# Gate logits and branch products with columns on partitions, and the merged sum split straight from SBUF

## The chip, the core and the metric

The kernel runs on one core of one Trainium2 chip. The metric is device time in microseconds (us), from launch to end, as the median of several runs. The engines are TensorE (PE; its weight loads are listed apart as PEld), VectorE (DVE), ScalarE (ACT), GpSimd (POOL) and SyncE (SP), which issues the large transfers.

## The reference

Two layers of a streaming encoder on x of 256 tokens by 2048 channels, all in float32. What bears on the change:

```python
proj = h @ w_in                       # 2048 -> 14400 columns
(rq, rk, rv, rg, lx, lg, mq, mkv, mkr, mg, merge_logits) = split(proj, ...)
gates  = sigmoid(merge_logits).reshape(256, 3, 2048)
merged = (gates[:, 0] * (y_ret @ w_branch[0:1024])
        + gates[:, 1] * (y_lru @ w_branch[1024:2048])
        + gates[:, 2] * (y_mla @ w_branch[2048:3072]))
y   = merged @ w_out
out = x + (1 + res_gate) * rms_norm(y, norm_post)
```

`h` is a normalised x, scaled and shifted by vectors that come from `silu(c) @ ada_w` (2048 by 6144 per layer; this sum is called ada below).

## The kernel before

**Products.** Every large product takes its weights in tiles of 256 rows by 1024 columns. A tile is one transfer of 1 MB on SP's queue into a buffer called raw (four of them, shared with the loads of ada_w). It is cut into two pieces of 128 rows by 1024 columns, kt 0 and kt 1. ACT rounds each piece to a 12-bit head, `wh` (line 291), and DVE subtracts the head to get the rest, `wl` (line 292). There are three `wh` and three `wl` buffers in all. The activation is kept in the same two parts, `h` and `l`. A product is the sum of three matmuls, wh by h, wh by l and wl by h.

A product can be made in two ways. With **tokens on partitions** (`gemm_x`, line 349) the activation is stationary and the weights are moving, 128 rows by 512 columns: 24 matmuls per tile. In the last tile of a group its steps are sorted by token half, so that the two PSUM banks of the first half are complete before those of the second. With **columns on partitions** (`gemm_w`, lines 367 to 369) the weights are stationary and the activation is moving, 128 by 256 tokens: 48 matmuls per tile, kt 0 first and kt 1 after it in every tile. A group is a product of 1024 columns. It takes four of the six PSUM banks called acc; two more banks, called mi, serve small work. Its results are read out of the four banks, an eviction for each: ACT by a copy (line 392) or a sigmoid (line 398), DVE by an add to a partial sum (line 394).

**Stages of a layer.** Layer 0 computes h in blocks of 2, 2, 4, 4 and 4 pieces of 128 channels, as its shift and scale become known, and after each block multiplies it into six groups called lx, lg, mqkv, mg, lru0 and lru1. In the first two blocks each group is thus a single tile, and in the other three it is two tiles. lx, lg and mg have columns on partitions. lru0 and lru1 are the two halves of the gate logits of the LRU branch and have, like all logits, tokens on partitions. The remaining products follow: those of retention and of MLA, with groups of 8 tiles, and the logits mla0, mla1, ret0, ret1. In layer 1 every group of `w_in` has 8 tiles. The six branch products (`branch`, 4 tiles each) multiply their PSUM banks by the gates on DVE (line 1047) and add them on POOL (line 1050). The sum is then transposed, 64 transposes of 128 by 128 through the mi banks (line 1105), and split into the two parts (lines 567 on ACT and 568 on DVE) for the product with `w_out`.

**Order.** PE and SP work in program order: small work (attention, transposes, sums over partitions) is called between tiles by `tick`. The order on ACT, DVE and POOL is made by a scheduler at build time, from priorities; casts and subtractions of weights come first (offset 400), then evictions (offset 300). On the chip each engine then works its list in order. The sums for ada (line 454 on DVE, line 445 on ACT, line 449 on POOL) run on tiles of ada_w beside the products: shift and scale of layer 0 during its first blocks, and its residual gate and the sums for layer 1 later, through the rest of layer 0.

Of the kernel before, what the change touches and what calls it, by code (L numbers as in the profile page):

```python
# [14 lines left out]
AF = mybir.ActivationFunctionType  # L15
# [4 lines left out]
P = 128  # L20
# [18 lines left out]
# per-layer vectors and their 128-blocks (ada_b: shift and scale only)  # L39
# [14 lines left out]
def hybrid_trunk(ctx: ExitStack, tc: tile.TileContext, a, out):  # L54
# [178 lines left out]
    def softplus_lambda(l):  # L233
        """8 * softplus(-lambda), and its negative"""
# [38 lines left out]
    def load_split(src, nk, ncol, spare=None):  # L273
        """heads and rests of a tile [128, nk, ncol], at most 1024 columns in a piece; in slots, listed in
        spare, if that is given"""
# [26 lines left out]
    class Act:  # L302
        """An operand [d, tokens], head and rest, in pieces of four d-tiles."""
# [21 lines left out]
    def gemm_x(act, w, r0, c0, kts, banks, ncol=W1, before=None, late=False):  # L325
        """tokens on partitions: banks[hf][j] += act.T @ w, the d-tiles in kts; yields after each tile.
        The first half of the tokens ends ahead of the second, by two tiles with late."""
# [25 lines left out]
    def gemm_w(act, w, r0, c0, kts, banks, before=None):  # L353
        """columns on partitions: banks[j][:, n, :] += w.T @ act for 8 blocks of 128 columns."""
        k_all = list(range(*kts))
        for k0 in k_all[::2]:
            nk = min(2, kts[1] - k0)
            if before is not None:
                before(k0)
            for k, (wh, wl) in enumerate(load_split(wsrc(w, r0, k0, nk, c0, W1), nk, W1)):  # L360
                kt = k0 + k
                for nb in range(8):
                    dst = banks[nb // 2][:, (nb % 2) * T:(nb % 2 + 1) * T]
                    cs = slice(nb * P, (nb + 1) * P)
                    first = kt == k_all[0] and nb % 2 == 0
                    last = kt == k_all[-1] and nb % 2 == 1
                    mm(dst, wh[:, cs], act.H(kt), start=first, stop=False, skip_group_check=True)  # L367
                    mm(dst, wh[:, cs], act.L(kt), start=False, stop=False, skip_group_check=True)  # L368
                    mm(dst, wl[:, cs], act.H(kt), start=False, stop=last, skip_group_check=True)  # L369
            yield  # L370
# [5 lines left out]
    def act_slice(res, i):  # L376
        """The i-th 512 columns of a result held in two slots."""
        return res[i // 2][:, (i % 2) * 512:(i % 2 + 1) * 512]

    def group(act, w, c0, mode, kts, res, func, partial, before):  # L380
        """One product of 1024 columns into two slots (res, if given): token halves, or blocks 0-3 and 4-7."""
# [28 lines left out]
    def mean_of(ss):  # L410
        """sum of the parts / D + eps"""
# [5 lines left out]
    def square(src, acc, vector=False):  # L417
        """acc: the row sums of src ** 2, 512 columns"""
# [43 lines left out]
    def ada_block(l, k0, k1, pause, share):  # L462
        """gain and shift of the d-tiles k0..k1"""
# [14 lines left out]
    def gains(l, scale, shift, k0, k1):  # L478
        """norm gain and shift of the d-tiles k0..k1 from the adaLN sums."""
# [17 lines left out]
    def ada_res(l):  # L497
        """(1 + res_gate) * norm_post on every partition, in pieces of 512 columns"""
# [762 lines left out]
```

## Time and profile before

| | |
|---|---|
| median of 3 runs (lowest, highest) | 2019.5 us (2019.4, 2023.18) |
| the profiled execution: span | 2016.0 us |
| its own time, span and what lies around it | 2019.5 us, the median, stands for it: 3.5 us lie outside the span |
| PE matmul busy | 1932.3 us, 96%, 9980 matmuls |
| PE weight loads busy | 1624.1 us, 81% |
| DVE busy | 1399.9 us, 69% |
| ACT busy | 991.0 us, 49% |
| POOL busy | 181.6 us, 9% |
| mean granted clock of TensorE | 0.991 |

The page gives one profiled execution. The span is the time from its first to its last instruction; the time of a run is longer by what lies ahead of and behind that. In a row of the timeline the first number is the start, the second the duration in us, and square brackets hold the idle time before the instruction and what ended it. A row with x2 or more stands for several instructions on end.

### The profile page before, as it was taken

How to read it: one execution, taken by the hardware profiler on the slowest of the kernel's cores; microseconds unless marked ns; L12 is line 12 of the kernel's file. 1: busy time of each engine (PE TensorE's matmuls, PEld its weight loads, DVE VectorE, ACT ScalarE, POOL GpSimd, SP SyncE). 2: the span in 40 equal slices, each digit the busy share in tenths (PEclk: the TensorE clock that was granted, in tenths of full speed). 3: DMA queues.
4: the chain of work that ended last, by engine and by line, in shares of the span. 5: the costliest groups of instructions: out<-in, count | busy, mean ns of one | idle time of the engine just before them, and what ended most of it. 6: DMA issues, size and time to landing. Idle time of an engine off the chain costs nothing.

```text
span 2016.0 us, 25350 instructions
## 1 busy us (share of the span) xinstructions
PE 1932.3 (96%) x9980; PEld 1624.1 (81%) x9980; DVE 1399.9 (69%) x1812; ACT 991.0 (49%) x1286; POOL 181.6 (9%) x137
## 2 busy tenths in 40 slices
PE   2979999999999999999989999999999999999998
PEld 2867888778988888777879989888898888788886
DVE  7899989787877687767567754446565447786555
ACT  5744538644554544433454774444455444444443
POOL 2242401100000010102010010000000001010100
PEclk9989999999999999999989999999999999999999
DMA  8787863787867777776655555555554557778563
GB/s 294 260 285 272 304 234 120 272 291 245 297 236 252 266 255 259 277 271 217 222 198 189 173 181 188 188 178 181 171 192 147 198 186 250 246 270 282 187 210 125
DMA packets 156936, 456.98 MB, mean 227 GB/s; under 512 B 12144, under 2 KB 20336, under 8 KB 156816
## 3 DMA queue, kind: packets, MB, share of 16 engines
q1 hardware_dynamic: 153248, 443.44, 64.8%
q0 software_dynamic: 3424, 11.65, 1.9%
q8 instruction: 78, 1.28, 0.3%
q14 instruction: 42, 0.34, 0.0%
q10 hardware_dynamic: 144, 0.26, 0.0%
HBM read 451.13 MB, written 4.19 MB: 226 GB/s over the span
## 4 chain that ended last, share of the span: by engine, by line
PE 79%; DVE 11%; DMA 6%; ACT 2%; issue 2%; POOL 0%; SPq 0%; DVEq 0%; ACTq 0%; POOLq 0%
PE acc L349 59%; DMA raw<-in_ada_w 5%; DVE float L454 4%; DVE wl L292 4%; PE acc L368 4%; PE acc L369 4%; PE acc L367 4%; DVE float L394 1%; PE mi L714 1%; PE mi L713 1%; PE mi L871 1%; ACT wh L291 0%; POOL float L891 0%; DMA raw<-in_w_in 0%; PE mi L801 0%
## 5 line engine op out<-in xcount | busy, mean ns | idle before, releaser
L349 PE MATMUL acc<-wh,float32r 128*128 128x512 f32 x4064 | 1159.4, 400 | 4.7 <-DVE float L394 4.4
L292 DVE TENSOR_TENSOR wl<-raw,wh 128x1024 fp32r<-128x1024 f32 (+1 forms) x640 | 794.0, 1244 | 451.9 <-ACT wh L291 445.4
L291 ACT CAST wh<-raw 128x1024 fp32r<-128x1024 f32 (+1 forms) x640 | 666.0, 1042 | 826.0 <-PE acc L349 656.2
L349 PEld LDWEIGHTS acc<-wh,float32r 128*128 128x128 f32 x4064 | 759.2, 189 | 186.3 <-DVE float L394 8.4
L349 PE MATMUL acc<-wl,float32r 128*128 128x512 f32 x2032 | 651.8, 397 | 13.8 <-DVE wl L292 13.8
L349 PEld LDWEIGHTS acc<-wl,float32r 128*128 128x128 f32 x2032 | 381.9, 189 | 110.6 <-DVE wl L292 20.6
L454 DVE SCALAR_TENSOR_TENSOR float<-raw,c_act,float 128x512 f32<-128x512 f32 (+1 forms) x326 | 255.7, 786 | 62.6 <-DMA raw<-in_ada_w 57.9
L367 PE MATMUL acc<-float32r,wh 128*128 128x256 f32 x768 | 218.7, 285 | 5.0 <-ACT float32r L567 5.0
L368 PE MATMUL acc<-float32r,wh 128*128 128x256 f32 x768 | 217.2, 283 | 0.8 <-DVE float32r L568 0.8
L369 PE MATMUL acc<-float32r,wl 128*128 128x256 f32 x768 | 217.1, 283 | 0.7 <-DVE wl L292 0.6
L367 PEld LDWEIGHTS acc<-float32r,wh 128*128 128x128 f32 x768 | 147.2, 192 | 6.3 <-ACT float32r L567 5.8
L368 PEld LDWEIGHTS acc<-float32r,wh 128*128 128x128 f32 x768 | 147.0, 191 | 1.8 <-DVE float32r L568 1.4
L369 PEld LDWEIGHTS acc<-float32r,wl 128*128 128x128 f32 x768 | 146.9, 191 | 1.1 <-DVE wl L292 1.1
L449 POOL TENSOR_TENSOR float<-float,float 128x512 f32<-128x512 f32 (+1 forms) x49 | 70.9, 1448 | 112.5 <-ACT float L445 107.5
L1050 POOL TENSOR_TENSOR float<-float,float 128x512 f32<-128x512 f32 x32 | 52.7, 1663 | 258.5 <-DVE float L1047 243.0
L394 DVE TENSOR_TENSOR float<-acc,float 128x512 f32<-128x512 f32 x96 | 62.5, 682 | 2.8 <-PE acc L349 1.4
L445 ACT ACTIVATE float<-raw,c_act 128x512 f32<-128x512 f32 (+1 forms) x64 | 40.1, 664 | 31.6 <-DMA raw<-in_ada_w 31.5
L793 POOL DMA_DIRECT2D float<-in_ret_gn x4 | 2.3, 570 | 570.0 <-PE mi L739 371.4
L470 PE MATMUL mi<-ident,float 128*128 128x128 f32 x64 | 10.4, 303 | 41.2 <-DVE float L458 41.2
L470 PEld LDWEIGHTS mi<-ident,float 128*128 128x128 f32 x64 | 8.1, 154 | 43.4 <-DVE float L458 42.5
L398 ACT ACTIVATE float<-acc 128x512 f32<-128x512 f32 x56 | 31.7, 598 | 13.0 <-PE acc L349 12.8
L1047 DVE TENSOR_TENSOR float<-acc,float 128x512 f32<-128x512 f32 x48 | 31.8, 683 | 2.4 <-PE acc L349 2.2
(231 smaller groups left out, 1286.2 us busy)
## 6 DMA issues: line engine op xcount, KB each, us to landing
raw<-in_w_in SPq DMA_DIRECT2D x224, 1024.0 KB, 5.1
raw<-in_ada_w SPq DMA_DIRECT2D x96, 1024.0 KB, 6.9
raw<-in_w_branch SPq DMA_DIRECT2D x48, 1024.0 KB, 6.2
raw<-in_w_out SPq DMA_DIRECT2D x32, 1024.0 KB, 5.5
raw<-in_mla_w_ukv SPq DMA_DIRECT2D x8, 1024.0 KB, 6.0
raw<-in_mla_w_uq SPq DMA_DIRECT2D x8, 768.0 KB, 4.5
float<-in_x SPq DMA_DIRECT2D x8, 512.0 KB, 7.5
float<-in_k_decay POOLq DMA_DIRECT2D x4, 512.0 KB, 4.5
```

Source lines behind the costliest of these rows:

```text
L291: nc.scalar.copy(wh, raw[:, c0:c0 + n])
L292: nc.vector.tensor_tensor(out=wl, in0=raw[:, c0:c0 + n], in1=wh.bitcast(F32), op=ALU.subtract)
L349: mm(b[:, 0:w_n], x, ws[:, j * w_n:(j + 1) * w_n], start=st, stop=sp)
L367: mm(dst, wh[:, cs], act.H(kt), start=first, stop=False, skip_group_check=True)
L368: mm(dst, wh[:, cs], act.L(kt), start=False, stop=False, skip_group_check=True)
L369: mm(dst, wl[:, cs], act.H(kt), start=False, stop=last, skip_group_check=True)
L394: nc.vector.tensor_tensor(out=dst, in0=b, in1=dst, op=ALU.add)
L445: nc.scalar.activation(out=t, in_=src, func=AF.Copy, scale=c)
L449: nc.gpsimd.tensor_tensor(out=acc[1], in0=acc[1], in1=t, op=ALU.add)
L454: nc.vector.scalar_tensor_tensor(acc[0], src, c, acc[0], ALU.mult, ALU.add)
L1047: nc.vector.tensor_tensor(out=gate[hf][:, cs], in0=banks[hf][j], in1=gate[hf][:, cs], op=ALU.mult)
L1050: nc.gpsimd.tensor_tensor(out=dst, in0=dst, in1=gate[hf][:, cs], op=ALU.add)
```

## The change

1. Gate logits: their six groups of 8 tiles per layer are made with columns on partitions (`m = "w"`) where they had tokens on partitions. The gate is then laid out with columns on partitions.
2. Branch products: their six groups of 4 tiles per layer go the same way, so that gates and products fit. Multiplications and additions stay as many, each of 128 by 512.
3. The merged sum now has channels on partitions. The 64 transposes go, and the split reads the sum from SBUF where it read PSUM.
4. `gemm_w` sorts the steps of its last tile by block of 128 columns: for each block kt 0, then kt 1. This holds for all groups with columns on partitions, lx, lg and mg among them. A group that is a single tile is sorted as a whole.

Over both layers, 3456 matmuls of 128 by 512 become 6912 of 128 by 256 (6 groups of 8 tiles and 6 of 4 per layer, 24 matmuls per tile before and 48 after). Comments and docstrings are left out too; below `gemm_w` the line numbers of the changed kernel are larger by two, and by one from `branch` on.

```diff
     def gemm_w(act, w, r0, c0, kts, banks, before=None):
         k_all = list(range(*kts))
         for k0 in k_all[::2]:
...
-            for k, (wh, wl) in enumerate(load_split(wsrc(w, r0, k0, nk, c0, W1), nk, W1)):
-                kt = k0 + k
-                for nb in range(8):
-                    dst = banks[nb // 2][:, (nb % 2) * T:(nb % 2 + 1) * T]
-                    cs = slice(nb * P, (nb + 1) * P)
-                    first = kt == k_all[0] and nb % 2 == 0
-                    last = kt == k_all[-1] and nb % 2 == 1
-                    mm(dst, wh[:, cs], act.H(kt), start=first, stop=False, skip_group_check=True)
-                    mm(dst, wh[:, cs], act.L(kt), start=False, stop=False, skip_group_check=True)
-                    mm(dst, wl[:, cs], act.H(kt), start=False, stop=last, skip_group_check=True)
+            steps = [(nb, k0 + k, ws) for k, ws in enumerate(load_split(wsrc(w, r0, k0, nk, c0, W1), nk, W1)) for nb in range(8)]
+            if k0 + nk > k_all[-1]:
+                steps.sort(key=lambda s: s[0])
+            for nb, kt, (wh, wl) in steps:
+                dst = banks[nb // 2][:, (nb % 2) * T:(nb % 2 + 1) * T]
...
-                c0, func, m = logits_col(*n), AF.Sigmoid, "x"
+                c0, func, m = logits_col(*n), AF.Sigmoid, "w"
...
-            banks = [[bank() for _ in range(2)] for _ in range(2)]
-            drive(gemm_x(acts[b], a["w_branch"][l], r0, c * W1, (0, 8), banks))
-            for hf in range(2):
-                for j in range(2):
-                    cs = slice(j * 512, (j + 1) * 512)
-                    nc.vector.tensor_tensor(out=gate[hf][:, cs], in0=banks[hf][j], in1=gate[hf][:, cs], op=ALU.mult)
-                    if order:
-                        dst = macc[hf][c][:, cs]
-                        nc.gpsimd.tensor_tensor(out=dst, in0=dst, in1=gate[hf][:, cs], op=ALU.add)
+            banks = [bank() for _ in range(4)]
+            drive(gemm_w(acts[b], a["w_branch"][l], r0, c * W1, (0, 8), banks))
+            for i, b_i in enumerate(banks):
+                g = act_slice(gate, i)
+                nc.vector.tensor_tensor(out=g, in0=b_i, in1=g, op=ALU.mult)
                 if order:
-                    release(gate[hf])
-                else:
-                    macc[hf][c] = gate[hf]
+                    dst = act_slice(macc[c], i)
+                    nc.gpsimd.tensor_tensor(out=dst, in0=dst, in1=g, op=ALU.add)
...
-        def turn_merged(c):
+        def split_merged(c):
             yield 1
-            for k in range(0, 8, 2):
-                b = mbank()
-                for i in range(2):
-                    for hf in range(2):
-                        nc.tensor.transpose(b[:, i * T + hf * P:i * T + (hf + 1) * P], macc[hf][c][:, (k + i) * P:(k + i + 1) * P], ident)
-                split_to(M, c * 8 + k, 2, b)
+            for i in range(4):
+                split_to(M, c * 8 + 2 * i, 2, act_slice(macc[c], i))
                 yield 1
```

The order of DVE moves with it. The first place is the last tile of the logits group ret1 in layer 0, at 892 us of the trace: its two pieces are `wl_7370` and `wl_7374` (raw_7367), and raw_7443 is a tile of ada_w. Before:

```order
L292 TENSOR_TENSOR wl_7328<-raw_7321,wh_7327 128x1024
L292 TENSOR_TENSOR wl_7370<-raw_7367,wh_7369 128x1024
L454 SCALAR_TENSOR_TENSOR float_11_87<-raw_7443,c_act,float_11_87 128x512 x2
L292 TENSOR_TENSOR wl_7374<-raw_7367,wh_7373 128x1024
L454 SCALAR_TENSOR_TENSOR float_11_87<-raw_7443,c_act,float_11_87 128x512 x2
L292 TENSOR_TENSOR wl_7412<-raw_7409,wh_7411 128x1024
```

Of the change, the same tile is raw_8879 with the pieces `wl_8882` and `wl_8886`, and raw_9003 is the same tile of ada_w:

```order
L292 TENSOR_TENSOR wl_8816<-raw_8809,wh_8815 128x1024
L292 TENSOR_TENSOR wl_8882<-raw_8879,wh_8881 128x1024
L456 SCALAR_TENSOR_TENSOR float_11_87<-raw_9003,c_act,float_11_87 128x512 x3
L292 TENSOR_TENSOR wl_8886<-raw_8879,wh_8885 128x1024
L456 SCALAR_TENSOR_TENSOR float_11_87<-raw_9003,c_act,float_11_87 128x512
```

Three ada steps stand ahead of the tile's second `wl` where two stood; the branch product ret0, at 917 us, moves in the same way.

The second place is DVE where a two-tile group lru1 ends and the next one begins, in layer 0 at 229 us (acc_1971 to acc_1974 are the banks of the group that has ended, raw_2115 and raw_2157 the next tiles). Before:

```order
L292 TENSOR_TENSOR wl_2048<-raw_2041,wh_2047 128x1024
L292 TENSOR_TENSOR wl_2118<-raw_2115,wh_2117 128x1024
L454 SCALAR_TENSOR_TENSOR float_6_82<-raw_2149,c_act,float_6_82 128x512 x2
L394 TENSOR_TENSOR float_19_95<-acc_1971,float_19_95 128x512
L292 TENSOR_TENSOR wl_2122<-raw_2115,wh_2121 128x1024
L394 TENSOR_TENSOR float_19_95<-acc_1972,float_19_95 128x512
L394 TENSOR_TENSOR float_20_96<-acc_1973,float_20_96 128x512
L292 TENSOR_TENSOR wl_2160<-raw_2157,wh_2159 128x1024
L394 TENSOR_TENSOR float_20_96<-acc_1974,float_20_96 128x512
```

Of the change, the banks are acc_2163 to acc_2166 and the next tiles raw_2307 and raw_2349:

```order
L292 TENSOR_TENSOR wl_2240<-raw_2233,wh_2239 128x1024
L292 TENSOR_TENSOR wl_2310<-raw_2307,wh_2309 128x1024
L396 TENSOR_TENSOR float_19_95<-acc_2163,float_19_95 128x512
L456 SCALAR_TENSOR_TENSOR float_6_82<-raw_2341,c_act,float_6_82 128x512
L396 TENSOR_TENSOR float_19_95<-acc_2164,float_19_95 128x512
L456 SCALAR_TENSOR_TENSOR float_6_82<-raw_2341,c_act,float_6_82 128x512
L396 TENSOR_TENSOR float_20_96<-acc_2165,float_20_96 128x512
L396 TENSOR_TENSOR float_20_96<-acc_2166,float_20_96 128x512
L292 TENSOR_TENSOR wl_2314<-raw_2307,wh_2313 128x1024
L292 TENSOR_TENSOR wl_2352<-raw_2349,wh_2351 128x1024
```

All four evictions now stand ahead of the next tile's second `wl`, where three of them stood behind it.

The third place is ACT at the end of the first single-tile group, lx of the first block, at about 50 us. raw_316 is the tile of the group after, and acc_232 to acc_235 are the banks of the group that ends. Before:

```order
L291 CAST wh_318<-raw_316 128x1024
L445 ACTIVATE float_15_91<-raw_374,c_act 128x256
L445 ACTIVATE float_18_94<-raw_374,c_act 128x256
L291 CAST wh_322<-raw_316 128x1024
L392 COPY float_16_92<-acc_232 128x512
L392 COPY float_16_92<-acc_233 128x512
L392 COPY float_17_93<-acc_234 128x512
L291 CAST wh_419<-raw_417 128x1024
```

Of the change:

```order
L291 CAST wh_318<-raw_316 128x1024
L447 ACTIVATE float_15_91<-raw_374,c_act 128x256
L447 ACTIVATE float_18_94<-raw_374,c_act 128x256
L394 COPY float_16_92<-acc_232 128x512
L394 COPY float_16_92<-acc_233 128x512
L394 COPY float_17_93<-acc_234 128x512
L291 CAST wh_322<-raw_316 128x1024
L291 CAST wh_419<-raw_417 128x1024
```

The cast of the next tile's second piece has moved behind three evictions.

## Rows read from the trace of the kernel before

**Rows 1.** The page, parts 1 and 4: busy time by engine; the chain's shares by engine.

```profile
PE 1932.3 (96%) x9980; PEld 1624.1 (81%) x9980; DVE 1399.9 (69%) x1812; ACT 991.0 (49%) x1286; POOL 181.6 (9%) x137
...
PE 79%; DVE 11%; DMA 6%; ACT 2%; issue 2%; POOL 0%; SPq 0%; DVEq 0%; ACTq 0%; POOLq 0%
```

**Rows 2.** Waits of PE: total us, times, longest.

```profile
PE acc L349 <- DVE wl L292: 13.8, 12, 2.4
```

**Rows 3.** Windows: stretch, us, busy PE, PEld, DVE, ACT, POOL, then clock, DMA share, GB/s.

```profile
96.00:115.00 19.00, 15.88 (x87) 12.95 (x86) 19.00 (x22) 7.16 (x10) 10.09 (x7) 1.00 0.64 217
115.00:131.00 16.00, 5.30 (x21) 3.63 (x19) 15.79 (x22) 6.72 (x9) 4.32 (x3) 0.69 1.00 351
...
1243.00:1332.00 89.00, 89.00 (x383) 71.71 (x382) 37.52 (x32) 38.62 (x43) 0.00 (x0) 1.00 0.54 176
```

**Rows 4.** Timeline of PE: starts of two tiles, of 24 and of 48 matmuls, and what follows each.

```profile
304.31 0.63 PE L349 MATMUL acc<-wh,float32r 128*128 128x512 f32 x2
...
309.90 1.89 PE L871 MATMUL mi<-float,float 128*128 128x256 f32 x8
...
324.54 0.28 PE L367 MATMUL acc<-float32r,wh 128*128 128x256 f32 x1
...
330.14 0.62 PE L349 MATMUL acc<-wh,float32r 128*128 128x512 f32 x2
```

**Rows 5.** Timeline of PE around four of the 64 transposes.

```profile
938.09 0.62 PE L349 MATMUL acc<-wh,float32r 128*128 128x512 f32 x2
938.55 0.60 PE L1105 MATMUL mi<-ident,float 128*128 128x128 f32 x4
938.90 0.71 PE L349 MATMUL acc<-wh,float32r 128*128 128x512 f32 x2
939.46 0.62 PE L349 MATMUL acc<-wl,float32r 128*128 128x512 f32 x2
```

**Rows 6.** Groups by line and shape, over the whole span: ACT's half of the split, by source.

```profile
L567 ACT CAST float32r<-float 128x512 fp32r<-128x512 f32 x15 | 9.3, 621 | 30.1 <-DVE float L559 30.1
L567 ACT CAST float32r<-mi 128x512 fp32r<-128x512 f32 x16 | 8.9, 581 | 0.2 <-PE mi L1105 0.2
```

**Rows 7.** Timeline of a calm tile: one weight piece through ACT and DVE.

```profile
838.22 1.05 ACT L291 CAST wh<-raw 128x1024 fp32r<-128x1024 f32 x1 [1.75 <-PE acc L349]
...
839.31 1.23 DVE L292 TENSOR_TENSOR wl<-raw,wh 128x1024 fp32r<-128x1024 f32 x1 [0.16 <-ACT wh L291]
```

**Rows 8.** Timeline of single-tile groups in layer 0: mg's start, its second rest; waits in lru0, lru1.

```profile
57.12 0.28 PE L367 MATMUL acc<-float32r,wh 128*128 128x256 f32 x1
...
59.65 1.21 DVE L292 TENSOR_TENSOR wl<-raw,wh 128x1024 fp32r<-128x1024 f32 x1
...
104.08 0.74 PE L349 MATMUL acc<-wl,float32r 128*128 128x512 f32 x2 [1.16 <-DVE wl L292]
...
111.84 0.73 PE L349 MATMUL acc<-wl,float32r 128*128 128x512 f32 x2 [1.89 <-DVE wl L292]
```

**Rows 9.** Timeline of PE behind the ends of two-tile groups in layer 0.

```profile
158.95 0.50 PE L349 MATMUL acc<-wh,float32r 128*128 128x512 f32 x1 [1.24 <-DVE float L394]
...
231.59 0.50 PE L349 MATMUL acc<-wh,float32r 128*128 128x512 f32 x1 [0.66 <-DVE float L394]
233.33 0.58 PE L349 MATMUL acc<-wh,float32r 128*128 128x512 f32 x1 [1.24 <-DVE float L394]
...
234.56 1.91 PE L349 MATMUL acc<-wh,float32r 128*128 128x512 f32 x4
...
237.08 1.09 PE L349 MATMUL acc<-wh,float32r 128*128 128x512 f32 x4
```

**Rows 10.** Timeline around the last tiles of ret1's logits and of the branch product ret0.

```profile
894.05 1.54 DVE L454 SCALAR_TENSOR_TENSOR float<-raw,c_act,float 128x512 f32<-128x512 f32 x2 [4.85 <-DMA raw<-in_ada_w]
...
896.77 0.73 PE L349 MATMUL acc<-wl,float32r 128*128 128x512 f32 x2 [1.61 <-DVE wl L292]
...
921.98 0.74 PE L349 MATMUL acc<-wl,float32r 128*128 128x512 f32 x2 [2.42 <-DVE wl L292]
```

More of the change, by code (lines that the diff above doesn't have):

```diff
@@ L359, in gemm_w @@
                 before(k0)
-            for k, (wh, wl) in enumerate(load_split(wsrc(w, r0, k0, nk, c0, W1), nk, W1)):
-                kt = k0 + k
-                for nb in range(8):
-                    dst = banks[nb // 2][:, (nb % 2) * T:(nb % 2 + 1) * T]
-                    cs = slice(nb * P, (nb + 1) * P)
-                    first = kt == k_all[0] and nb % 2 == 0
-                    last = kt == k_all[-1] and nb % 2 == 1
-                    mm(dst, wh[:, cs], act.H(kt), start=first, stop=False, skip_group_check=True)
-                    mm(dst, wh[:, cs], act.L(kt), start=False, stop=False, skip_group_check=True)
-                    mm(dst, wl[:, cs], act.H(kt), start=False, stop=last, skip_group_check=True)
+            steps = [(nb, k0 + k, ws) for k, ws in enumerate(load_split(wsrc(w, r0, k0, nk, c0, W1), nk, W1)) for nb in range(8)]
[3 more added lines that the diff above has]
+                dst = banks[nb // 2][:, (nb % 2) * T:(nb % 2 + 1) * T]
+                cs = slice(nb * P, (nb + 1) * P)
+                first = kt == k_all[0] and nb % 2 == 0
+                last = kt == k_all[-1] and nb % 2 == 1
+                mm(dst, wh[:, cs], act.H(kt), start=first, stop=False, skip_group_check=True)
+                mm(dst, wh[:, cs], act.L(kt), start=False, stop=False, skip_group_check=True)
+                mm(dst, wl[:, cs], act.H(kt), start=False, stop=last, skip_group_check=True)
             yield
@@ L965, in layer @@
         acts = {}
-        macc = [[None, None] for _ in range(2)]
+        macc = [None, None]
         freed = set()
@@ L1041, in branch @@
             r0 = BRANCH[b] * W1
-            banks = [[bank() for _ in range(2)] for _ in range(2)]
-            drive(gemm_x(acts[b], a["w_branch"][l], r0, c * W1, (0, 8), banks))
-            for hf in range(2):
-                for j in range(2):
-                    cs = slice(j * 512, (j + 1) * 512)
-                    nc.vector.tensor_tensor(out=gate[hf][:, cs], in0=banks[hf][j], in1=gate[hf][:, cs], op=ALU.mult)
-                    if order:
-                        dst = macc[hf][c][:, cs]
-                        nc.gpsimd.tensor_tensor(out=dst, in0=dst, in1=gate[hf][:, cs], op=ALU.add)
-                if order:
-                    release(gate[hf])
-                else:
-                    macc[hf][c] = gate[hf]
+            banks = [bank() for _ in range(4)]
[3 more added lines that the diff above has]
+                nc.vector.tensor_tensor(out=g, in0=b_i, in1=g, op=ALU.mult)
+                if order:
+                    dst = act_slice(macc[c], i)
+                    nc.gpsimd.tensor_tensor(out=dst, in0=dst, in1=g, op=ALU.add)
+            if order:
+                release(*gate)
+            else:
+                macc[c] = gate
             if c == 1:
@@ L1097, in layer @@
         M = Act(NKT)
-        def turn_merged(c):
+        def split_merged(c):
             yield 1
-            for k in range(0, 8, 2):
-                b = mbank()
-                for i in range(2):
-                    for hf in range(2):
-                        nc.tensor.transpose(b[:, i * T + hf * P:i * T + (hf + 1) * P], macc[hf][c][:, (k + i) * P:(k + i + 1) * P], ident)
-                split_to(M, c * 8 + k, 2, b)
+            for i in range(4):
+                split_to(M, c * 8 + 2 * i, 2, act_slice(macc[c], i))
                 yield 1
-            release(macc[0][c], macc[1][c])
-        start("m0", turn_merged(0))
+            release(*macc[c])
+        start("m0", split_merged(0))
         branch("ret", 1, 2)
         finish("m0")
-        start("m1", turn_merged(1))
+        start("m1", split_merged(1))
         def before(k0):
```

## The prediction

> **What bounds the kernel now.** I read the page first. PE is busy for 96% of the span and makes 79% of the chain that ended last; DVE makes 11% of it, with 69% busy [rows 1]. So the end moves by what PE does and by where PE stands still. Next I read windows, since a mean over stages hides the second part. In layer 1 a calm stretch of 89 us has PE busy throughout and DVE for 37.5 us: nothing but matmul time counts there. In the first 131 us it is the other way round: DVE is busy 19.00 of 19 us and then 15.79 of 16, while PE works 5.30 of those 16 at a mean clock of 0.69 [rows 3]. Last I read the waits of PE and the timelines where they stand. The longest list in the products is PE waiting for a rest `wl`, 13.8 us in 12 waits [rows 2]: few, and nearly all in layer 0, where the ada work shares DVE.
>
> **The converted matmuls themselves: 0.** A tile with tokens on partitions runs from 304.31 to 309.90, a tile with columns on partitions from 324.54 to 330.14 [rows 4]. That is 5.59 and 5.60 us for the same columns, so 0.233 us per matmul of 512 columns and 0.117 per matmul of 256. The 3456 converted matmuls become 6912 at half the time each, with twice the weight loads, all hidden in the tile shown. Nothing is to be gained or lost by the count.
>
> The Trainium skill, "TensorE: Matmul & The Clock Gate", section "Back-to-back issue gap", says that the spacing of matmuls is set by weight load and matmul together, and gives for one matmul alone a fixed 2.5 ns beside the time of its columns; by that the 3456 extra ones would cost about 8.6 us, an estimate from the page. The trace shows no such addition in a tile of 48.
>
> **The transposes: -7.0.** From 938.09 to 939.46 there are four matmuls of 512 columns and four transposes, 1.37 us [rows 5]. Four such matmuls alone take 4 x 0.233 = 0.93. So a group of four transposes costs 0.44 on PE, and 16 groups 7.0. They stand between matmuls of a PE that doesn't wait there, so all of it should be gained; the bounds are 6.5 to 7.5, for the spread of the modelled ends. ACT's part of the split takes 621 ns from SBUF and 581 from PSUM [rows 6]: 16 x 0.04 = 0.6 us on an engine at half load, hidden behind PE's tiles.
>
> **The sorted last tile.** Its six matmuls per block of 128 columns take 6 x 0.117 = 0.70 us. Four effects follow.
>
> Its banks are complete at 1.4, 2.8, 4.2 and 5.6 us, where an unsorted one has them at 3.5, 4.2, 4.9 and 5.6 and a converted group had two at 2.8 and two at 5.6. So evictions are spread out and only the last is left after the tile.
>
> It wants the second piece early. Its sixth matmul takes the second `wl`, at 5 x 0.117 = 0.58 us after its start. An unsorted one wants that at 2.80 + 0.23 = 3.03, a sorted one with tokens on partitions at 8 x 0.233 = 1.87.
>
> It holds its first piece for long, to 5.25 us (unsorted 2.80, the other kind 4.20). The tile after it takes that buffer for its own second piece, since there are three. ACT and DVE need 839.31 + 1.23 - 838.22 = 2.32 us for a piece [rows 7], and I take 2.5 with what lies between freeing and start. So that piece is ready 5.25 + 2.5 - 5.6 = 2.15 us into the next tile. An ordinary next tile wants it at 3.03 or 3.27 and doesn't wait. A next tile that is sorted itself waits 2.15 - 0.58 = 1.6.
>
> In calm stretches a last tile that follows an ordinary one has its second piece before its start (2.80 + 2.5 - 5.6 = -0.3), so it doesn't wait: 0 for layer 1 but for one place.
>
> **Blocks 0 and 1 of layer 0: +4.8.** Here every group is one tile, and five of six are sorted as wholes. The 1.6 us stands at lx to lg, mg to lru0, lru0 to lru1 and lru1 to the next lx; 0.3 at lg to mqkv and 0.5 at mqkv to mg (4.20 + 2.5 - 5.6 = 1.1, less 0.58). Over two blocks that is 4 x 1.6 + 0.8 in the first, 3 x 1.6 + 0.8 in the second, 12.8 in all. The rows agree that pieces are late: mg starts at 57.12 and its second rest ends at 59.65 + 1.21 = 60.86, 3.74 into the tile. Waits of 1.16 and 1.89 at lru0 and lru1 of the second block stand there already [rows 8]; counted off, 9.8 are left. Behind them lies the stretch from 115 to 131 in which PE mostly waits for DVE. A late PE is free there as long as DVE isn't held up by it; DVE is held where a `wl` waits in its list for a cast, and ACT's cast now stands behind evictions (third place of the order). Bounds: 0, if DVE keeps its pace, and 9.8, if all is passed on. With DVE without slack and PE with 10, I take the middle, 4.8.
>
> **Blocks 2 to 4: -3.5.** Waits for evictions go. The rows show 1.24 at 158.95, then 0.66 and 1.24, and behind that a stretch at half clock: from 233.33 to 237.08 nine matmuls take 3.75 us where 9 x 0.233 = 2.10 is due [rows 9]. Four matmuls take 1.91 there and 1.09 at the end of it, so the clock had fallen from 2.4 to 1.2 GHz behind those waits, for 1.65 us. Sum 4.8. In their place, all four evictions stand ahead of the next tile's second `wl` (second place of the order). The last starts when the tile ends; with 0.68 for it, up to one ada step of 0.77 [rows 10] and 1.2 for `wl`, that is ready after 2.0 to 2.9 us against 3.03 or 3.27: covered, barely. Where DVE is late by another 1 us, the three blocks pay up to 3 waits of 1 for this and, with last tiles that want 0.58, as much again. Bounds -8 (all small waits go too, four more of the same kind) and +3; I take -4.8 plus 1.3 for new waits.
>
> **The ada stage later in layer 0: +3.** At 894.05 DVE starts two ada steps, having stood 4.85 us for their transfer, while the `wl` of a last tile is behind them in its list; PE then waits 1.61. The branch product at 917 does the same, 2.42 [rows 10]. Five last tiles stand like this (mla1, ret0, ret1 and the branch ret0 of layer 0, mla1 of layer 1). Each wants its piece 1.87 - 0.58 = 1.3 earlier than now, and at two of them a third ada step, 1.54 / 2 = 0.77, now stands ahead (first place of the order). At worst 5 x 1.3 + 2 x 0.77 = 8. But the transfer is late against PE, and once one wait has put PE back, the next one shrinks. Bounds 0.5 and 8; I take 3.
>
> **Sum.** -7.0 + 4.8 - 3.5 + 3.0 = -2.7. The profiled span of 2016.0 becomes 2013.3, and with the 3.5 outside it, as in the median of 2019.5, the time is 2016.8: **2017 us**. About 0.2%, 4 us, is what a measurement of this kernel can tell from no change, so faster means under 2015.5 and slower above 2023.5.
>
> **Rivals.** *A, edges hidden (27%).* Blocks 0 and 1 end in the idle stretch and cost nothing, the ada stage costs its 0.5, and the evictions give their 4.8: 2019.5 - 7.0 - 4.8 + 0.5 = 2008. For it: PE has 10 us to spare before 131. Against it: DVE has none.
>
> *B, slower: three buffers are too few (25%).* A tile that wants both pieces at once, with a third buffer only, makes PE wait at each edge. The full 9.8 of blocks 0 and 1 is passed on through DVE, the ada stage pays 6, and in blocks 2 to 4 new waits equal the old: -7.0 + 9.8 + 6 + 0 = +8.8, about 2028. It decides as soon as such waits exceed 7 + 4 = 11 us over what goes. For it: 3.74 us of lateness in rows 8. Against: later tiles are calm.
>
> The Trainium skill, "Perfetto Trace Analysis", section "Optimization Strategy", names repeated gaps on the engine that should be saturated as a possible sign of too few buffers for the next tile. The waits at 104.08 and 111.84 would be of that kind; the calm stretch of layer 1 shows none.
>
> *C, the shorter matmuls cost more than their columns in a long run (7%).* Groups of 8 such tiles hardly stand in layer 0's blocks, where the cadence was read; 1 ns more for each of 6912 would be +7, and 2017 would become 2024. Against: 48 in a row keep 0.117.
>
> **Chances.** The forecast has 41%, its own range 2011 to 2022, and about two fifths of it lie under 2015.5. A is faster throughout, nearly; B and C are mostly slower. Faster 0.27 + 0.15 = 0.42, same 0.33, slower 0.25. From A's 2008 with 1 to spare to B's 2028, the range leaves out about 2 in 10: 2007 to 2028.
>
> **What would show it.** Line 1105 is gone and the tiles around 940 take 5.60 again. A tile of converted logits in layer 1 takes 5.60; if it takes more, C holds. Between 45 and 115, PE waits for `wl` behind each single-tile group, some 1.6 each; block 2 then starts at 131 (A) or up to 10 us later (B). At 157 and 231 no wait for an eviction and no half clock. Last tiles near 890 and 920 wait 2 to 4 us. The forecast is wrong if the scheduler's order delays a `wl` in a place that is calm now, or if the wait for shift and scale before block 2 grows with PE.

## The result, and the profile after

The changed kernel takes 2040.59 us (median of 4 runs, 2034.95 to 2044.25) against 2021.34 for the kernel before beside it. The ratio is 1.0096, interval 1.0076 to 1.0117: slower by 15 to 24 us, outside the range of 2007 to 2028. The profiled execution has a span of 2038.4 us, 22.4 more than before.

The page, parts 1 and 4, of the changed kernel (as [rows 1] of before):

```profile
PE 1938.0 (95%) x13372; PEld 1786.2 (88%) x13372; DVE 1398.9 (69%) x1812; ACT 992.7 (49%) x1286; POOL 182.3 (9%) x137
...
PE 74%; DVE 12%; DMA 8%; issue 3%; ACT 2%; POOL 1%; SPq 0%; DVEq 0%; ACTq 0%; POOLq 0%
```

DVE's work is what it was, 1398.9 us against 1399.9. PE is busy for 5.7 us more, though the transposes are gone (half clock, told below, has its part in that), and stands still for 16.7 us more (100.4 us of the span against 83.7). In the waits of PE (as [rows 2]: total, times, longest), the waits for a rest `wl` have grown from 14.4 us in 13 (the row of [rows 2] and one wait of 0.6 at line 369) to 35.7 in 34:

```profile
PE acc L371 <- DVE wl L292: 29.2, 25, 3.5
...
PE acc L349 <- DVE wl L292: 6.5, 9, 1.2
```

Calm stretches are as forecast. The timeline of PE has a converted tile of the logits in layer 1, of the group lru0, from 1270.17 to 1275.77, 5.60 us for 48 matmuls:

```profile
1270.17 0.28 PE L369 MATMUL acc<-float32r,wh 128*128 128x256 f32 x1
...
1275.77 0.28 PE L369 MATMUL acc<-float32r,wh 128*128 128x256 f32 x1
```

Where the time went is read best from the starts of the same tile in both traces. The table has the starts on PE, in us, of the first tile of block 2, of the last tile of the blocks (lru1), of the first tile of the logits mla0, of the second tile of the branch product ret1, of the first tile of layer 1, of the second tile of its branch product mla0, and of the last tile but one; experiments told below are in it too. Each row is one execution, and runs of one kernel lie up to 9 us apart (2034.95 to 2044.25 for the change), so a step of 2 or 3 us in a single row proves nothing by itself.

```
                             block 2  blocks' last          mla0          ret1       layer 1     mla0 of 1  last but one
before                         130.7         350.6         658.8         933.0        1052.2        1678.0        1996.4
change                         146.0         370.3         676.7         956.1        1072.9        1701.4        2019.0
e1_unsorted                    130.4         347.6         655.8         938.9        1055.0        1680.7        1999.5
e2_sort_long                   130.6         352.8         658.9         941.2        1058.0        1686.1        2006.1
e4_before_sort                 136.0         356.8         665.4         940.5        1059.8        1686.3        2005.9
e8_after_lead                  146.6         370.1         676.1         964.9        1081.7        1710.2        2031.2
e9_before_no_ada_dma           131.7         351.4         659.3         928.1        1047.3        1673.0        1988.3
e11_after_no_ada_dma           142.3         370.7         677.9         949.7        1066.6        1693.2        2007.8
e12_four_buffers               131.8         357.1         668.1         957.6        1073.3        1699.0        2011.5
e13_unsorted_queue             129.9         346.4         654.2         923.2        1039.6        1665.3        1978.0
e14_before_queue               131.0         349.1         656.4         924.1        1043.3        1669.0        1984.2
e15_after_queue                144.0         367.4         673.1         942.2        1059.0        1685.7        2000.4
```

By the last column the change is 22.6 us behind. 15.3 are lost before block 2 begins, 4.4 in blocks 2 to 4 (1.8 come back behind them), and 5.2 between mla0 and ret1, where ada_w is loaded beside the logits. The end of layer 0 gives 2.4 back, layer 1 loses 2.7 by its mla0, and 0.8 come back behind that.

The first of these stretches, in windows of the changed kernel (columns as [rows 3]); 28 to 146 reaches to the start of block 2:

```profile
28.00:146.00 118.00, 87.95 (x558) 79.86 (x558) 98.50 (x148) 58.83 (x90) 30.93 (x23) 0.91 0.72 250
...
64.00:67.00 3.00, 3.00 (x17) 3.00 (x16) 0.00 (x0) 1.40 (x7) 0.00 (x0) 0.54 0.95 323
117.00:130.00 13.00, 9.19 (x53) 8.78 (x52) 11.96 (x13) 4.81 (x7) 7.98 (x6) 0.74 0.48 168
```

The same stretch of the kernel before, to the start of its block 2:

```profile
28.00:131.00 103.00, 78.95 (x465) 67.97 (x465) 95.56 (x148) 58.12 (x89) 28.84 (x22) 0.95 0.80 276
```

DVE, whose busy time is the third in these rows, has the same 148 instructions. It is busy 98.5 us for 95.6, and not busy for 19.5 us where it was for 7.4. Busy and not busy always add up to the length of a stretch; what the two say is that of the 15 us added, 2.9 are work of DVE and 12.1 are DVE standing still. The waits in that stretch say for what, two rows of DVE's and one of ACT's, changed kernel:

```profile
DVE wl L292 <- ACT wh L291: 7.6, 4, 6.5
DVE float L396 <- PE acc L371: 4.1, 5, 1.0
...
ACT wh L291 <- PE acc L370: 16.2, 9, 5.2
```

Before, the first of them was 2.6 us, the second was not there, and the largest row like the third was 5.7 (line 368). So DVE, with the least slack in these blocks, now waits for heads that ACT can't cast before PE frees a buffer, and for banks that PE fills late.

One such tile in the timeline of the changed kernel, mg of the first block (as [rows 8]):

```profile
59.67 1.98 ACT L291 CAST wh<-raw 128x1024 fp32r<-128x1024 f32 x2
59.89 0.28 PE L369 MATMUL acc<-float32r,wh 128*128 128x256 f32 x1
60.75 0.38 PE L369 MATMUL acc<-float32r,wh 128*128 128x256 f32 x1 [0.35 <-ACT wh L291]
61.64 2.35 DVE L292 TENSOR_TENSOR wl<-raw,wh 128x1024 fp32r<-128x1024 f32 x2
62.91 0.38 PE L371 MATMUL acc<-float32r,wl 128*128 128x256 f32 x1 [1.66 <-DVE wl L292]
...
69.58 0.28 PE L369 MATMUL acc<-float32r,wh 128*128 128x256 f32 x1
```

The tile takes 69.58 - 59.89 = 9.69 us. 5.60 is work and 0.35 + 1.66 are the two waits, first for the head of the second piece, then for its rest. About 1.7 of the other 2.08 is the clock: from 63.3 to 66.7 PE runs at half clock (from 64 to 67 the mean granted clock is 0.54, that is 1.2 GHz for nearly all of it), and PE is busy throughout. The rest stands at the two waits, since the idle time in brackets begins only at the modelled end of the matmul before. The late tile then holds up DVE: its longest wait for a head, 6.46 us, ends at 70.45, and the cast that it waits for began at 69.37, when PE had freed a buffer. The longest wait of PE for a rest stands in the group lru0 of the second block:

```profile
119.91 4.43 DVE L292 TENSOR_TENSOR wl<-raw,wh 128x1024 fp32r<-128x1024 f32 x2
...
122.18 0.58 PE L371 MATMUL acc<-float32r,wl 128*128 128x256 f32 x1 [3.49 <-DVE wl L292]
```

Three stretches at half clock lie between 63 and 129 of the changed kernel, 17 us together, where PE has work. Before, PE fell to half clock in these blocks only in the idle stretch of [rows 3], where it had next to none. In both kernels the half clock of the idle stretch reaches into block 2, for 4.0 us before and for 6.0 in the change, which makes about 1 us of the loss in blocks 2 to 4.

PE's waits for rests and heads from 28 to 146, changed kernel:

```profile
PE acc L371 <- DVE wl L292: 10.1, 8, 3.5
...
PE acc L369 <- ACT wh L291: 2.7, 7, 0.7
PE acc L349 <- DVE wl L292: 1.5, 2, 1.1
```

That is 14.3 us; before it was 4.0 (3.4 at line 349, 0.6 at line 369). PE is also busy for 9.0 us more by the windows above, and the three stretches at half clock, in which it is busy for 15.5 us, make some 7.7 of that.

In blocks 2 to 4 the timeline of PE has no wait for an eviction at the places of [rows 9], but others in their place:

```profile
175.28 0.73 PE L349 MATMUL acc<-wh,float32r 128*128 128x512 f32 x2 [0.71 <-ACT wh L291]
176.70 0.73 PE L349 MATMUL acc<-wl,float32r 128*128 128x512 f32 x2 [0.69 <-DVE wl L292]
...
240.17 0.38 PE L371 MATMUL acc<-float32r,wl 128*128 128x256 f32 x1 [2.34 <-DVE wl L292]
```

The first two stand in the tile behind the group lg of block 2, whose last tile is sorted; the third in the first tile of lg in block 3, behind the sorted last tile of lx. Behind this third wait PE is at half clock from 240.8 to 244.2, as long as it was behind the evictions of [rows 9]. (The second place of the order shown ahead of the prediction, at 229 us, is the end of lg too, and was named lru1 there by mistake.)

### The profile page after: what moved, and what is told of

It is laid out like the page before. It is cut to its first block, busy times and chain, and to the rows that moved or that the text cites. A ratio compares the mean times of both kernels' runs of the same rounds, so it can differ in the third digit from the quotient of the medians.

```text
span 2038.4 us, 32237 instructions
## 1 busy us (share of the span) xinstructions
PE 1938.0 (95%) x13372; PEld 1786.2 (88%) x13372; DVE 1398.9 (69%) x1812; ACT 992.7 (49%) x1286; POOL 182.3 (9%) x137
## 4 chain that ended last, share of the span: by engine, by line
PE 74%; DVE 12%; DMA 8%; issue 3%; ACT 2%; POOL 1%; SPq 0%; DVEq 0%; ACTq 0%; POOLq 0%
PE acc L349 27%; PE acc L371 13%; PE acc L370 13%; PE acc L369 13%; DMA raw<-in_ada_w 7%; DVE wl L292 5%; DVE float L456 3%; ACT wh L291 1%; DVE float L396 1%; PE mi L716 1%; PE mi L715 1%; PE mi L873 1%; DVE float32r L570 0%; PE acc L682 0%; PE acc L689 0%
## 5 line engine op out<-in xcount | busy, mean ns | idle before, releaser
L371 PE MATMUL acc<-float32r,wl 128*128 128x256 f32 x3072 | 867.0, 282 | 29.2 <-DVE wl L292 29.2
L369 PE MATMUL acc<-float32r,wh 128*128 128x256 f32 x3072 | 875.3, 285 | 11.2 <-ACT float32r L569 8.2
L370 PE MATMUL acc<-float32r,wh 128*128 128x256 f32 x3072 | 864.9, 282 | 0.9 <-DVE float32r L570 0.9
L371 PEld LDWEIGHTS acc<-float32r,wl 128*128 128x128 f32 x3072 | 584.8, 190 | 34.5 <-DVE wl L292 34.2
L369 PEld LDWEIGHTS acc<-float32r,wh 128*128 128x128 f32 x3072 | 585.0, 190 | 16.5 <-ACT float32r L569 9.2
L370 PEld LDWEIGHTS acc<-float32r,wh 128*128 128x128 f32 x3072 | 584.8, 190 | 4.3 <-issue 1.9
L349 PE MATMUL acc<-wh,float32r 128*128 128x512 f32 x1760 | 504.5, 398 | 0.7 <-ACT wh L291 0.7
L349 PEld LDWEIGHTS acc<-wh,float32r 128*128 128x128 f32 x1760 | 327.5, 188 | 76.8 <-ACT wh L291 1.1
L349 PE MATMUL acc<-wl,float32r 128*128 128x512 f32 x880 | 286.9, 396 | 6.5 <-DVE wl L292 6.5
L456 DVE SCALAR_TENSOR_TENSOR float<-raw,c_act,float 128x512 f32<-128x512 f32 (+1 forms) x326 | 251.0, 772 | 61.2 <-DMA raw<-in_ada_w 56.5
L349 PEld LDWEIGHTS acc<-wl,float32r 128*128 128x128 f32 x880 | 164.6, 188 | 49.4 <-DVE wl L292 10.4
L569 ACT CAST float32r<-float 128x512 fp32r<-128x512 f32 (+1 forms) x33 | 20.0, 607 | 56.3 <-DVE float L561 29.5
```

The costliest lines, as they stand in the source:

```text
L349: mm(b[:, 0:w_n], x, ws[:, j * w_n:(j + 1) * w_n], start=st, stop=sp)
L456: nc.vector.scalar_tensor_tensor(acc[0], src, c, acc[0], ALU.mult, ALU.add)
```

## The experiments

Two theories were tested. **S**, formed from this: the sorted last tile costs. It wants both pieces at once and, with three buffers, keeps the next tile's second piece from being made; the waits lower the clock. **W**, formed after e1: in the later stage DVE stands in its list for tiles of ada_w, with rests behind. The rivals M and K say that columns on partitions cost in themselves. Times are compared with runs of the kernel before on the same chip, five rounds each.

**The sort taken apart.** e1 drops it, e2 keeps it for groups of more than one tile, e3 sorts by halves, e4 puts it alone into the kernel before.

```diff
             if k0 + nk > k_all[-1]:                       the change, two lines
                 steps.sort(key=lambda s: s[0])
-            (both lines left out)                         e1_unsorted
+            if k0 + nk > k_all[-1] and len(k_all) > 2:    e2_sort_long
+                steps.sort(key=lambda s: s[0] // 4)       e3_sort_pairs
+            (both lines put into the kernel before)       e4_before_sort
```

> The change without the sort of the last tile; all else stays. Theory S (the sorted last tile is what costs: it wants both pieces at once, and with three buffers each for heads and rests it holds one of them to its end; the waits then let TensorE's clock fall): the 15 us lost by the start of block 2 come back, and the 5 or so of the later last tiles, the gain of the transposes stays: 2012 to 2016 us, 5 to 9 under the kernel before. Rival M (columns on partitions for logits and branch products costs in itself, by its 6912 short matmuls or by the order that the scheduler makes of it): it stays slower than the kernel before, 2025 to 2040.

> The change, with the sort only in groups of more than one tile; the single-tile groups of blocks 0 and 1 work kt 0 first, then kt 1. Theory S, if single tiles are the place: block 2 starts near 131 as before, what is left are the late last tiles beside the ada work, +5 to +8, against -7 for the transposes: 2019 to 2026. If long groups pay most, or rival M holds: 2033 to 2041.

> The change, with the last tile sorted by halves of four column blocks: kt 0 and kt 1 of the blocks 0 to 3, then of 4 to 7. The second rest is wanted 1.6 us after the tile's start (0.6 sorted in full, 3.0 unsorted), and the first piece's buffer is free at 4.2 of 5.6 (5.25 and 2.8). Theory S: the waits shrink by what the two numbers say, nearly all of those after single tiles go: 2013 to 2022. Rival M: no better than the change, 2033 to 2041.

> The kernel before with the sorted last tile alone, which acts on lx, lg and mg of both layers; logits, branch products and transposes as before. Theory S: six sorted single tiles in blocks 0 and 1 where the change has ten, and six last tiles in blocks 2 to 4 and layer 1: 5 to 12 us slower than the kernel before, 2026 to 2033. Rival M: within 3 us of the kernel before.

| | us | ratio to before, interval |
|---|---|---|
| e1_unsorted | 2020.73 | 1.0001, 0.9990 to 1.0012 |
| e2_sort_long | 2027.46 | 1.0036, 1.0023 to 1.0049 |
| e3_sort_pairs | 2023.71 | 1.0014, 1.0004 to 1.0024 |
| e4_before_sort | 2027.53 | 1.0035, 1.0021 to 1.0048 |

S holds for the loss: without the sort, block 2 starts at 130.4 and all of the change's excess over the kernel before is gone. By e2, single tiles make some 12 of the 19 us (ratios 1.0096 and 1.0036) and long groups 7 (1.0036 and 1.0001). By e3, wanting the second rest at 1.6 us and freeing the first piece at 4.2 costs only 3, with an interval that overlaps e1's. The sort alone, on lx, lg and mg, costs the kernel before 7 us, as expected; e2 and e3 came out 1.5 and 1.7 above the ranges expected of them. But e1 missed its number by 5 to 9, and stayed 4 under that of rival M: it is no faster than the kernel before, though the transposes are gone. The table of starts shows where it loses: at mla0 it is 3.0 us ahead, at ret1 5.9 behind.

**The transposes alone, and a later call of the ada steps.** e5 is the kernel before with the merged sum split without being transposed, which leaves that part of the computation out. e6 to e8 call the ada steps one weight tile later than their load, in e1, in the kernel before and in the change.

```diff
-            for k in range(0, 8, 2):
-                b = mbank()
...
-                        nc.tensor.transpose(b[:, ...], macc[hf][c][:, ...], ident)
-                split_to(M, c * 8 + k, 2, b)
+            for i in range(4):
+                split_to(M, c * 8 + 2 * i, 2, macc[i // 2][c][:, (i % 2) * 512:(i % 2 + 1) * 512])
```

```diff
                 raw = load_raw(ada_rows[l][:, r0:r0 + nr, c0:c0 + ncol], nr, ncol)
+                if pause == 2:
+                    yield 1
...
-                yield pause
+                yield 1
```

> The kernel before with the 64 transposes left out: the merged sum is split straight from SBUF with tokens still on partitions, so the product with w_out gets it untransposed. Tokens on partitions stay everywhere else, no sort. It prices the transposes alone. Forecast's term: 7.0 us less than the kernel before, 2012 to 2014. Rival G (the time is given back in another wait behind them): within 3 us of the kernel before.

> The change without the sort, and with the ada steps behind the layer-0 blocks (both for the residual gate and for layer 1) called one tile later than the load that they wait for. Theory W (in the ada stage of layer 0 DVE stands in its list for a tile of ada_w and the rests of the weights stand behind it, which costs the unsorted version the gain of the transposes): the 5 to 9 us lost between 655 and 960 come back, 2008 to 2016. Rival (the loss there is the short matmuls' own or the evictions'): as without this edit, 2018 to 2023.

> The kernel before with the same later call of the ada steps. Theory W: it gains what it loses itself in that stage, the waits of 1.6 and 2.4 us and one stretch at half clock, 4 to 8 us: 2012 to 2017, and it stays 5 to 8 us above the unsorted version with the same edit. Rival: no difference, 2018 to 2022.

> The change as it is, sort and all, with the same later call of the ada steps. Theory S and W together: the loss of blocks 0 and 1 (15 us) stays, since these steps are not touched there, the 5 of the ada stage goes: 2031 to 2036. If the ada steps of the later stage were all of the loss: 2020. If they have no part in it: 2038 to 2043.

e5 takes 2014.73, ratio 0.9962 (0.9950 to 0.9974): 5 to 10 us less, as the term of 7.0 said. So e1 gives these 7 back elsewhere. e6 (2021.63, ratio 1.0000, 0.9989 to 1.0010) and e7 (2022.93, 1.0009, 0.9999 to 1.0020) changed nothing, but they didn't test W: in e6 DVE still waits 87.8 and 24.2 us for ada_w at the two lines of the ada steps, in e1 81.8 and 24.9. e8 went the wrong way by 11 to 12 us, 2052.48 (1.0149, 1.0135 to 1.0163). By the table it loses 9.4 us more than the change between mla0 and ret1 and 3.4 more behind mla0 of layer 1, at both of which ada_w is loaded, and DVE's waits for ada_w at the two lines are 81.4 and 20.8 us where the change has 56.5 and 13.8. That fits W: the later call made its loss larger.

**Without the loads of ada_w; and a fourth buffer.** e9 to e11 are the kernel before, e1 and the change with the 64 later loads of ada_w left out: the ada steps read their own sum, so the modulation of layer 1 and the residual gates are not computed. e12 is the change with four buffers for heads and rests, and three for raw.

```diff
+                if pause == 2:
+                    for i in range(nr):
+                        if r0 + i == 0:
+                            nc.vector.memset(acc[0], 0.0)
+                        else:
+                            nc.vector.scalar_tensor_tensor(acc[0], acc[0], ada_scalar(r0 + i), acc[0], ALU.mult, ALU.add)
+                    yield pause
+                    continue
                 raw = load_raw(ada_rows[l][:, r0:r0 + nr, c0:c0 + ncol], nr, ncol)
```

> The kernel before, in which the ada steps behind the layer-0 blocks keep their place and number on DVE but read their own sum instead of tiles of ada_w, whose 64 loads are left out (the modulation of layer 1 and both residual gates come out as constants). It is the control for the next two. Theory W (DVE stands in its list for tiles of ada_w, rests of weights behind it): it loses its own such waits, 4 to 10 us: 2011 to 2017.

> The change without the sort, and without the loads of ada_w behind the blocks, as in the control. Theory W (what the unsorted version gives back of the transposes' 7 us is lost to late tiles of ada_w in layer 0's logits): it is 5 to 9 us below the control. Rival K (columns on partitions for logits and branch products cost that in themselves, by short matmuls or evictions): within 3 us of the control.

> The change with its sort, without the loads of ada_w behind the blocks. Theories S and W: what is left of the sort's price is that of blocks 0 and 1, where loads of ada_w stay, 15 us, less 7 for the transposes: 6 to 10 us above the control. If late last tiles of long groups cost without these loads too: 12 to 20 above it.

> The change, with four buffers each for heads and rests where it has three, and three raw buffers where it has four (for room). The second piece of a tile no longer takes the buffer of the last tile's first piece but that of its forerunner. Theory S, as far as it says that the third buffer is what binds: the 1.6 us behind each single tile go, 2022 to 2030. If what binds is DVE and ACT, busy with ada in these blocks, or the raw buffer that is gone costs as much: 2036 to 2050.

Control e9: 2010.74. e10: 2005.07, 5.7 less, so with nothing to wait for the gain of the transposes shows, and rival K falls. e11: 2028.55, 17.8 above the control, where S had 6 to 10: late last tiles of long groups cost without these loads too. By the table 10.6 stand before block 2, 8.7 in blocks 2 to 4, which lie ahead of these loads, and 3.0 between mla0 and ret1. e12: 2032.02, ratio 1.0050 (1.0035 to 1.0066), half of the change's loss. Its block 2 starts at 131.8 and not at 146.0, so in blocks 0 and 1 the third buffer is what binds. ACT's waits for PE ahead of a cast are 2.7 us there and not 16.2, and PE's first stretch at half clock begins at 120.0, in the idle stretch. The rest is lost later, above all between mla0 and ret1 (9.3 behind at the one, 24.6 at the other), in a kernel with one raw buffer less; whether that buffer is the reason was not tested. In all, e12 came out 2 us above the range expected.

**DVE's order, with all loads kept.** A scheduling edge, which orders an engine's list and makes nothing wait for a result, queues the ada steps behind the rest `wl` that stands ahead of them in the program (`last_wl[0]` is the last subtraction of line 292). It is put into e1 (e13), the kernel before (e14) and the change (e15); e16 is e13 with the later call.

```diff
+                with ExitStack() as order:
+                    if pause == 2:
+                        order.enter_context(tc.issue_after(last_wl[0]))
+                    for i in range(nr):
...
```

> The change without the sort; the ada steps behind the layer-0 blocks stand in DVE's list behind the second rest of the weight tile ahead of them, by a scheduling edge without a wait. All loads and all work stay. Theory W (rests stand behind ada steps that wait for their transfer): the 5 to 9 us that the unsorted version gives back in layer 0's logits return, 2010 to 2016, under both kernels. Rival (it is the traffic of ada_w itself that costs, and not DVE's order): as without the edge, 2018 to 2024.

> The kernel before with the same edge, as control. Theory W: it loses its own waits behind ada steps, 3 to 9 us: 2012 to 2018, and stays 3 to 8 above the unsorted version with the edge. Rival: 2018 to 2024.

> The change as it is, with the same edge. Theories S and W: the ada part goes, the sort's part stays, 16 to 24 us above the unsorted version with the edge, 2028 to 2036. If what the sort costs behind block 1 hangs on DVE's order alone: 2022 to 2028.

> As the unsorted version with the edge, and each group of ada steps called one weight tile later than its load. Theory W: as with the edge alone or up to 3 us less. If a raw buffer that is held for longer costs more than the order gives: 2016 to 2026.

| | us | ratio to before, interval |
|---|---|---|
| e13_unsorted_queue | 2001.21 | 0.9900, 0.9887 to 0.9914 |
| e14_before_queue | 2007.59 | 0.9932, 0.9920 to 0.9945 |
| e15_after_queue | 2019.58 | 0.9994, 0.9985 to 1.0003 |
| e16_unsorted_queue_late | 2000.69 | 0.9899, 0.9885 to 0.9912 |

W holds, by DVE's order and not by the traffic, which is the same with the edge. e1, without the edge, in its timeline between mla0 and ret1:

```profile
863.59 0.75 DVE L454 SCALAR_TENSOR_TENSOR float<-raw,c_act,float 128x512 f32<-128x512 f32 x1 [5.28 <-DMA raw<-in_ada_w]
864.25 1.22 DVE L292 TENSOR_TENSOR wl<-raw,wh 128x1024 fp32r<-128x1024 f32 x1
...
865.53 0.39 PE L369 MATMUL acc<-float32r,wl 128*128 128x256 f32 x1 [2.63 <-DVE wl L292]
```

DVE stands 5.28 us for a tile of ada_w, the rest that PE wants is next in the list, and PE waits 2.63. Between mla0 and ret1 PE waits 8.5 us in e1, 4.0 before and 0.4 in e13, and it is at half clock for 10.2, 3.4 and 0 us. One of e1's three waits is not for a rest: small work waits 3.89 us for ACT at 750.60, and with the edge 0.43 of that is left. DVE's waits for ada_w in e1 over the whole span:

```profile
DVE float L454 <- DMA raw<-in_ada_w: 81.8, 33, 6.0
DVE float L452 <- DMA raw<-in_ada_w: 24.9, 11, 3.6
```

Before, the same two rows have 57.9 and 16.3. From mla0 to just behind ret1 the two kernels differ little, 43.0 us in e1 and 39.6 before: what costs there is less how long DVE waits in sum than what stands behind it in the list. With the edge, in e13, one wait of the kind is left:

```profile
DVE float L456 <- DMA raw<-in_ada_w: 2.6, 1, 2.6
```

With all loads kept, the unsorted version is 6.4 us below the kernel before with the same edge, which is the transposes, and 20 below the kernel before itself; e16's later call adds nothing that can be told. The unsorted version with the edge is the one that beats both kernels. The differences between e13, e14 and e15 are as expected, but all three times are lower than expected, by 9, 4 and 8 us: W costs more than was thought, in the kernel before too. Against e1, e13 gains 14.1 us between mla0 and ret1, and 6.1 behind mla0 of layer 1, where the residual gate of layer 1 is summed from ada_w, a place that W as put here leaves out. The sort's price is 18.4 us with the edge (e15 against e13); by the table 14.1 stand before block 2 and 6.9 in blocks 2 to 4; from there to ret1 none is added.

## Why the prediction was wrong, step by step

**The converted matmuls, 0.** Right: 5.60 us per tile after. Rival C falls.

**The transposes, -7.0.** Right as their price: 7.0 in e5, 6.4 between e13 and e14. In the change itself 2.4 of it shows at the end of layer 0 and 0.8 behind mla0 of layer 1. Layer 1, which the forecast had at 0 but for one place, loses 2.7 ahead of that; 1.36 us of it is a wait for a rest at 1698.03, where ada_w is loaded again.

**Blocks 0 and 1, +4.8, bounds 0 and 9.8.** This step failed. It had the mechanism of rival B, buffers and a second piece wanted at 0.58 us, and the price was 15.3. The waits themselves came as counted: 10.3 us more than before (14.3 against 4.0), where the prediction had 9.8. Two things were missing. The first is the clock: the prediction priced half clock behind evictions [rows 9], and not behind the new waits. It makes 7.7 us of PE time here; mg pays about 1.7 for it on top of 2.01 of waits. The second is the middle between "absorbed" and "passed on". The idle 10 us of PE before block 2 are DVE's working time, so a wait of DVE for a head or a bank moves block 2: DVE stands still for 12.1 us more and block 2 starts 15.3 later. With 19.0 of 19 us busy in [rows 3], DVE had no slack to share, and the upper end, not the middle, was nearest to that row. e12 shows that the third buffer is the cause and e2 that single tiles are the place.

**Blocks 2 to 4, -3.5.** This step failed too, in sign: +4.4, beyond the bound of +3 (+2.6 with what comes back behind them). The waits for evictions went as said, 4.4 us, but 1.3 for new waits was far too little: waits for rests and heads grew from 0.9 us to 9.1. The last tiles of mg and one of lx, which want their second rest at 0.58 us, got it 1.5 to 1.8 us after their start, and a tile behind a sorted one as late as 5.6, where the prediction had 2.0 to 2.9 (its own terms make 1.9 to 2.7). The half clock did not go either; it moved behind the wait at 240.17. Without the sort (e1) the blocks gain 2.7 (217.2 against 219.9 us from the first column to the second): waits for evictions are 3.0 us there, and no half clock follows them.

**The ada stage, +3, bounds 0.5 and 8.** Between mla0 and ret1 the change loses 5.2, inside the bounds. The waits do stand in last tiles, as said. But the cause was not the early piece: e1, without sorted tiles, loses 8.9 there, in other tiles, and with the edge the sort adds nothing (269.1 us from mla0 to ret1 in e15, 269.0 in e13 and 267.7 in e14). It is DVE's new order around ada steps, in any tile, that costs; the three steps ahead of a rest (first place of the order) were a sign of it that was priced for two last tiles alone.

**The chances.** B had the right side and the right place with 25%, and its 2028 was 12 too low. It passed the 9.8 us of blocks 0 and 1 on in full, which the waits bear out, but without the clock; it set new waits in blocks 2 to 4 equal to the old, and they cost more; and it counted all 7.0 of the transposes, of which 3.2 show in the change.

## What to carry to other kernels

Sorting the last tile of a product so that its banks end early moves a need for operands forward and the release of a buffer back. Before doing it, count buffers against the tile after, above all in groups of a single tile. Where one engine works in order for two consumers, put work that waits for a late transfer behind the work that the busiest engine waits for: here an edge in the scheduler was worth 13 us in the kernel before, twice what the transposes were. And price a wait of PE with the half-clock stretch that can follow it, and a wait of a saturated engine in full.

## What the runs showed of the hardware

In the changed kernel waits of 0.35 and 1.66 us in one tile are followed by half clock from 63.3 to 66.7. The wait of 3.49 us that ends at 122.18 has half clock from 121.3 to 128.1. Not every wait has it: of the two in [rows 10], 1.61 us at 896.77 is followed by none, and 2.42 at 921.98 by half clock from 923.1 to 926.5. Two subtractions at 119.91 take 4.43 us where two take 2.35 at 61.64; GpSimd adds from 119.78 to 123.25 beside the first two and does nothing beside the others. That this is the reason was not tested.
